# Turning attention probabilities by two row halves of the tensor engine instead of whole blocks

## The chip, the core and the metric

The kernel runs on one of the eight cores of a Trainium2 chip. A core has five engines that run side by side and meet at semaphores: TensorE (PE, with its weight loads listed apart as PEld), VectorE (DVE), ScalarE (ACT), GpSimd (POOL) and SyncE (SP), whose queue issues the DMA transfers here. TensorE multiplies a stationary operand, loaded as weights, with a moving operand and writes into PSUM, which has eight banks of 128 partitions by 512 float32. VectorE and ScalarE read PSUM and write SBUF.

The metric is the device time of one execution in microseconds. Three runs of the kernel before took 1234.39, 1236.35 and 1236.84 us; the median is 1236.35 us.

## What is computed

One layer of a decoder trunk for 1024 tokens of width 1024, batch 1, all in float32: a normalised input goes through one combined projection; a gated delta rule with four heads (mixer A) and a dilated attention with eight heads of 64 (mixer B) run on its columns; both outputs go through one output projection; then a gated MLP with a short convolution and a final norm. The change is in mixer B:

```python
DIL_PATTERNS = ((128, 1), (512, 4), (2048, 16))
for window, dil in DIL_PATTERNS:       # query t sees t, t-d, ..., t-window
    num, den, m = band_attention(stride(qf), stride(kf), stride(vf), window // dil)
# the three branches are merged by their softmax denominators
out = num_tot / den_tot[..., None]
```

So each query sees near keys (its own block of 128 tokens and the block before it), and further keys only where the distance is a multiple of 4 or of 16. The kernel computes the three branches as one softmax with a mask that adds the logarithm of how many branches see a key.

## The kernel before, in words

A small planner (`Weave`) holds the kernel's parts as Python generators with a level each, and a model of when every tile will be ready. `wv.need(...)` tells how long TensorE should do other work before a tile is ready; `wv.run` then always continues the stream of lowest level that is due. The order in which products are recorded is the order in which TensorE executes them (`mm` at L188 and `tp` at L192 stamp it). The planner thereby fills dense projections (`mm3`, three products of 128x512 for each pair of high and low parts of a float32 matrix) between the small pieces of the attention. Each product has a planned duration, an argument of `mm`; a transpose (`tp`) is planned at 0.11 us. Waits that remain on the chip are semaphore waits of the engine in question.

Attention goes over four head pairs (`pi`), two halves of the tokens (`hh`) and, in each, two pairs of query blocks of 128 tokens, so 16 pairs of blocks. In a block, token 4u+c stands at place 32c+u, so a residue class c mod 4 is 32 places in a row. For each pair of blocks `advance` (L1004) runs these steps, the first one for the pair before the current one:

- `turn` (L946): the probabilities `sm` (queries on partitions; the columns are first the far keys, 64 for every two blocks, then 128 or 256 near keys) are transposed, so that keys lie on partitions. Each 128x128 block of `sm` is the stationary operand of one `tp`, and the 128x128 identity the moving one. For each block of the pair and each of two heads there is one PSUM bank, with the near key tiles first and the far key tiles behind. VectorE copies the near part to `pt`; ScalarE copies the far part to `pb`.
- `scores` (L904): products of 64 rows (one head) by queries and near keys, one head in the upper and one in the lower half of the rows, then products with 32 columns for the far keys of each residue class; `softmax` (L929) subtracts the largest, takes exponentials and divides, on VectorE and ScalarE.
- `values` (L966): near probabilities `pt` times the near values `vn`, both heads into the two halves of the bank `po`.
- `merge_classes` (L975), after the second pair: far probabilities `pb`, kept for four blocks, times the far values `vc`, by residue class.

Banks are named by tags with two buffers each: `asc` and `atr` serve scores and transposes, `ch` the outputs `po`, `hf` the dense projections. A new bank of a tag waits for the readers of the bank two turns earlier. Engines take their instructions in order; `uv` and `ua` record VectorE and ScalarE work of the attention at raised priority. While attention runs, TensorE also does the remaining input projections (`dense`, L478: columns `a` and `z`) and the first products of the output projection (`out_proj`, L1069). In the profile, the transposes carry line L193, other products L189, the helper's engine calls L139 and L141.

Of the kernel before, what the change touches and what calls it, by code (L numbers as in the profile page):

```python
# [9 lines left out]
AF = mybir.ActivationFunctionType  # L10
# [5 lines left out]
P = 128  # L16
# [16 lines left out]
TOKEN = "pe"  # L33
# [4 lines left out]
PSLACK = 0.5  # L38
TSLACK = -1.0, -0.6
# [105 lines left out]
def hybrid_layer(tc, I, out):  # L145
    nc = tc.nc
    wv = Weave()
# [3 lines left out]
    uv = Engine(wv, nc.vector, "vector", 0.07, 0.00105, first=tc.high_priority)  # L151
    ua = Engine(wv, nc.scalar, "scalar", 0.12, 0.00085, first=tc.high_priority)
# [10 lines left out]
    def tile_(pool, shape, dt, name, tag, bufs):  # L163
        return wv.slot(pool.tile(list(shape), dt, name=name, tag=tag, bufs=bufs), tag, bufs)
# [12 lines left out]
    def const(name, shape, src=None):  # L177
        t = cp.tile(list(shape), F32, name=name)
        if src is not None:
            sy.dma_start(t, src)  # L180
        return t
# [6 lines left out]
    def mm(dst, lhs, rhs, us, start=True, stop=True, **kw):  # L188
        tc.stamp_issue_order_token(nc.tensor.matmul(dst, lhs, rhs, start=start, stop=stop, **kw).ins, TOKEN)  # L189
        wv.product(us, dst, lhs, rhs)  # L190

    def tp(dst, src):  # L192
        tc.stamp_issue_order_token(nc.tensor.transpose(dst, src, ident).ins, TOKEN)  # L193
        wv.product(0.11, dst, src)

    def mm3(dst, lhs, rhs, first, last, **kw):
        us = 0.2135 * rhs[0].shape[-1] / 512
# [46 lines left out]
    def bank(tag, name="ps"):  # L244
        return tile_(pp_, (P, 512), F32, name, tag, 2)
# [10 lines left out]
    def v8(t):  # L256
        return t.rearrange("p (c t) -> p c t", c=NCH)
# [53 lines left out]
    ident = const("ident", [P, P], I["ident"])  # L311
# [564 lines left out]
    def att_load(pi):  # L876
        qT, kT = [A(nm, "uy") for nm in ("qT", "kT")]
        for i, t in enumerate((qT, kT)):
            sy.dma_start(t, apark[pi, i])
        vn, vc = A("vn", "kt"), A("vc", "kt")  # L880
        cols = slice(pi * P, (pi + 1) * P)
        by_class = vpark.rearrange("(n u c) d -> c u n d", n=NCH, c=4)
        for c in range(4):
            sy.dma_start(v8(vn)[32 * c:32 * c + 32], by_class[c][:, :, cols])
        rows = vpark.rearrange("(b p c) d -> b p c d", b=2, c=4)
        for b in range(2):
            sy.dma_start(vc.rearrange("p (b c d) -> p b c d", b=2, c=4)[:, b], rows[b][:, :, cols])
        return qT, kT, vn, vc

    HALVES = (slice(0, 64), slice(64, 128))  # L890

    def attention():
# [51 lines left out]
                uv.tensor_scalar(sm[:, e, :wd], sm[:, e, :wd], den[:, e:e + 1], None, op0=OP.mult)  # L944

        def turn(pair):  # L946
            pts = A("pt", "dv*", shape=(P, 4, 256))
            for b, (it, tag) in enumerate(zip(pair, ("asc", "atr"))):
                sm, near, far = it["sm"], it["near"], it["far"]
                nf = -(-far // P)  # L950
                it["pt"] = []
                for e in range(2):
                    pt = pts[:, 2 * b + e, :]
                    it["pt"].append(pt)
                    pp = bank(tag)
                    yield wv.need(pp, sm, slack=TSLACK[b])
                    for i in range(near // P):
                        tp(pp[:, i * P:(i + 1) * P], sm[:, e, far + i * P:far + (i + 1) * P])
                    for i in range(nf):
                        tp(pp[:, near + i * P:near + (i + 1) * P], sm[:, e, i * P:(i + 1) * P])  # L960
                    uv.tensor_copy(pt[:, :near], pp[:, :near])
                    if nf:
                        ua.activation(it["pb"][e][:, it["u"], :nf, :].rearrange("p b t -> p (b t)"),
                                      pp[:, near:near + nf * P], AF.Copy)

        def values(pair):  # L966
            yield wv.need(pair[0]["po"], *pair[0]["pt"], slack=-PSLACK)
            for it in pair:
                u = it["u"]
                for i in range(it["near"] // P):  # L970
                    for e, er in enumerate(HALVES):
                        mm(it["po"][er, u * P:(u + 1) * P], v8(it["vn"])[:, it["k0"] // P + i, er],
                           it["pt"][e][:, i * P:(i + 1) * P], 0.11, u == 0 and i == 0, False, skip_group_check=True)

        def merge_classes(g):  # L975
            vcv = g["vc"].rearrange("p (b c d) -> p b c d", b=2, c=4)
            po, hh = g["po"], g["hh"]
            yield wv.need(*g["pb"], slack=-PSLACK)


            parts = (((0, 128, 0), (1, 64, 2)) if hh else ((0, 64, 2),))
            for c in range(4):
                for b, rows, u in parts:
                    for e, er in enumerate(HALVES):
                        mm(po[er].rearrange("p (u t) -> p u t", u=4)[:, u:, 32 * c:32 * c + 32],
                           vcv[:rows, b, c, er], g["pb"][e][:rows, u:, b, 32 * c:32 * c + 32], 0.11 - 0.028 * u,
                           False, c == 3 and b == hh, skip_group_check=True)

        def give(g):
# [14 lines left out]
        def advance(pair):  # L1004
            done = pipe.pop() if pipe else None
            if done is not None:
                yield from turn(done)
            if pair is not None:
                yield from scores(pair)
                pipe.append(pair)  # L1010
            if done is not None:
                yield from values(done)
                if done[1]["u"] == 3:
                    yield from merge_classes(done[0]["g"])
                    give(done[0]["g"])

        for pi in range(4):
            q, k, vn, vc = cur
            for hh in range(2):
                if hh == 1 and pi < 3:  # L1020
                    yield from wv.until(("a", pi + 1, 1))
                    cur = att_load(pi + 1)
                po = bank("ch")
                pb = [A("pb", "qa", shape=(P, 4, 1 + hh, P)) for _ in range(2)]
                if pi == 3 and hh == 1:
                    wv.done.add("last group")
                g = dict(po=po, pb=pb, hh=hh, pi=pi, vc=vc)
                for u in (0, 2):
                    yield from advance([dict(n=4 * hh + i, u=i, q=q, k=k, vn=vn, po=po, pb=pb, g=g)
                                        for i in (u, u + 1)])  # L1030
# [529 lines left out]
```

## Time and profile before

The profiled execution took 1232.33 us; its span from first to last instruction is 1230.2 us.

| | busy us | share of span | instructions |
|---|---|---|---|
| PE (products) | 1206.7 | 98% | 6848 |
| PEld (weight loads) | 992.2 | 81% | 6848 |
| DVE | 948.1 | 77% | 1522 |
| ACT | 570.7 | 46% | 1099 |
| POOL | 47.9 | 4% | 34 |

Busy time counts when at least one instruction of the engine was under way. Products are pipelined and overlap each other: two rows of TensorE may start 0.23 us apart and last 0.39 us each. What a product costs is therefore read from the starts of the products behind it, not from its length. In a row of the timeline the first number is the start in us, the second the length of the group, then engine, line and operation, output <- inputs, the tile of the array in rows*columns (128*128 is the whole array, 64*128 a half of its rows), the moving operand's or result's shape, and the count. A bracket tells how long the engine was idle before and what released it; "issue" means that the profile shows nothing that it waited for. A row of the tile view gives the shortest, middle and longest length in ns, and the first and last start. A row of the waits gives the total in us, the count and the longest.

### The profile page before, as it was taken

To read this page: it belongs to the slowest core of one execution; us is meant where nothing else is said; L and a number is where in the kernel's file an instruction comes from. 1 tells how busy PE (TensorE), PEld (TensorE's weight loads), DVE (VectorE), ACT (ScalarE), POOL (GpSimd) and SP (SyncE) were. 2 spreads that over 40 slices of the span, in tenths; PEclk is the share of its full clock that TensorE was granted. 3 is DMA by queue.
4 is the path that set the end of the run, shared out by engine and by line. 5 is a ranking of instruction groups with operands and counts; after the bars stand their busy time and mean duration, and the time that the engine had idled before them with its cause. 6 is when DMAs were issued, how large, how long until landed. Compare 5 with 4: busy or idle time off the path is not lost.

```text
span 1230.2 us, 17841 instructions
## 1 busy us (share of the span) xinstructions
PE 1206.7 (98%) x6848; PEld 992.2 (81%) x6848; DVE 948.1 (77%) x1522; ACT 570.7 (46%) x1099; POOL 47.9 (4%) x34
## 2 busy tenths in 40 slices
PE   9999999999999998999999999999999999999996
PEld 7878887888877776788888888888888888788886
DVE  7675964566377768577888889889898889899875
ACT  7393344356343345455544445444454553344441
POOL 0211010003100000000000000000000000000000
PEclk9999999999999999999999999999999999999998
DMA  6325251345722403343232231231322397545623
GB/s 231 104 90 154 83 154 71 122 136 167 238 74 95 121 27 111 129 153 117 74 103 88 66 103 61 94 101 53 103 76 79 108 373 254 172 153 183 195 86 137
DMA packets 85798, 155.02 MB, mean 126 GB/s; under 512 B 21168, under 2 KB 36176, under 8 KB 85712
## 3 DMA queue, kind: packets, MB, share of 16 engines
q1 hardware_dynamic: 85712, 153.87, 38.7%
q8 instruction: 54, 0.88, 0.3%
q14 instruction: 32, 0.26, 0.1%
HBM read 117.91 MB, written 35.93 MB: 125 GB/s over the span
## 4 chain that ended last, share of the span: by engine, by line
PE 83%; DVE 9%; DMA 4%; issue 2%; ACT 2%; POOL 0%; SPq 0%; POOLq 0%; DVEq 0%; ACTq 0%
PE ps L189 43%; PE pa L189 18%; PE pc L189 9%; PE dw L189 9%; PE ps L193 3%; DVE pr L139 2%; DMA wd<-in_wd 2%; DMA r<-upark 1%; DVE x1h L139 1%; DVE wd L139 1%; DVE kT L139 1%; DVE sm L141 1%; ACT dec L139 1%; PE warm L189 1%; DVE r L139 0%
## 5 line engine op out<-in xcount | busy, mean ns | idle before, releaser
L189 PE MATMUL dw<-pr 128*128 128x512 f32 (+1 forms) x984 | 213.2, 377 | 2.6 <-DVE x1h L139 1.9
L189 PEld LDWEIGHTS dw<-pr 128*128 128x128 f32 x984 | 176.1, 188 | 38.7 <-DVE x1h L139 3.6
L189 PE MATMUL ps<-xhi,whi 128*128 128x512 f32 x384 | 160.1, 417 | 0.0
L189 PE MATMUL ps<-xhi,wlo 128*128 128x512 f32 x384 | 150.5, 392 | 0.0
L189 PE MATMUL ps<-xlo,whi 128*128 128x512 f32 x384 | 150.1, 391 | 0.0
L189 PE MATMUL pa<-T,pair 128*128 128x512 f32 x528 | 127.0, 389 | 0.0
L189 PEld LDWEIGHTS pa<-T,pair 128*128 128x128 f32 x528 | 99.0, 188 | 20.5
L189 PEld LDWEIGHTS ps<-xhi,wlo 128*128 128x128 f32 x384 | 72.2, 188 | 16.1 <-DVE wlo L139 0.3
L189 PEld LDWEIGHTS ps<-xhi,whi 128*128 128x128 f32 x384 | 72.4, 189 | 14.9 <-issue 2.6
L189 PEld LDWEIGHTS ps<-xlo,whi 128*128 128x128 f32 x384 | 72.6, 189 | 11.2
L139 ACT ACTIVATE u<-pa 128x512 f32<-128x512 f32 x44 | 26.3, 598 | 110.7 <-PE pa L189 110.7
L139 DVE SCALAR_TENSOR_TENSOR y<-xu,fcw,y 128x1023 f32<-128x1023 f32 (+1 forms) x44 | 56.4, 1281 | 25.7 <-ACT y L139 25.6
L139 ACT ACTIVATE whi<-wst 128x1024 fp32r<-128x1024 f32 (+2 forms) x42 | 42.9, 1022 | 69.7 <-PE ps L189 64.1
L141 ACT ACTIVATE sm<-sm,mx 128x320 f32<-128x320 f32 (+4 forms) x64 | 36.1, 565 | 63.1 <-DVE mx L141 63.1
L189 PE MATMUL pc<-B,pair 128*128 128x512 f32 x264 | 63.4, 389 | 0.0
L189 PE MATMUL pa<-B,A 128*128 128x512 f32 x264 | 63.4, 389 | 0.0
L189 PE MATMUL pc<-T,S 128*128 128x512 f32 x264 | 63.4, 389 | 0.0
L189 PE MATMUL pa<-T,S 128*128 128x512 f32 x264 | 63.4, 389 | 0.0
L139 DVE TENSOR_TENSOR wst<-wst 128x512 f32<-128x512 f32 x88 | 60.4, 687 | 0.7
L189 PE MATMUL ps<-B,pair 128*128 128x512 f32 x252 | 60.5, 389 | 0.0
L139 DVE TENSOR_TENSOR wlo<-wst,whi 128x1024 fp32r<-128x1024 f32 (+2 forms) x42 | 49.4, 1175 | 12.1 <-ACT whi L139 12.0
L189 PEld LDWEIGHTS pa<-B,A 128*128 128x128 f32 x264 | 49.6, 188 | 10.3
(237 smaller groups left out, 2347.9 us busy)
## 6 DMA issues: line engine op xcount, KB each, us to landing
wst<-in_wu SPq DMA_DIRECT2D x44, 512.0 KB, 3.8
wd<-in_wd SPq DMA_DIRECT2D x44, 512.0 KB, 3.9
upark<-y SPq DMA_DIRECT2D x22, 512.0 KB, 3.8
wst<-in_wi SPq DMA_DIRECT2D x21, 512.0 KB, 3.7
r<-upark SPq DMA_DIRECT2D x11, 512.0 KB, 8.0
r<-upark SPq DMA_DIRECT2D x22, 256.0 KB, 7.0
wa<-in_wd SPq DMA_DIRECT2D x22, 256.0 KB, 2.8
wst<-in_wv SPq DMA_DIRECT2D x8, 512.0 KB, 3.6
```

The lines of the kernel that those rows point to most:

```text
L139: return getattr(eng, op)(*a, **kw)
L141: return getattr(eng, op)(*a, **kw)
L189: tc.stamp_issue_order_token(nc.tensor.matmul(dst, lhs, rhs, start=start, stop=stop, **kw).ins, TOKEN)
L193: tc.stamp_issue_order_token(nc.tensor.transpose(dst, src, ident).ins, TOKEN)
```

## The change

In `turn`, each transpose of a 128x128 block becomes two transposes with 64 rows: the upper and the lower 64 queries of the block, each with the matching 64x64 part of the identity, one after the other. The two halves write two banks, one per query half; a bank now holds both heads, with the key tiles of each. So two banks are taken at once and filled together, where each bank was filled for one head and copied before. A half is planned at 0.055 us. VectorE copies from each bank the near tiles of both heads for 64 queries. ScalarE copies each far tile of a bank by itself, both heads together. `pb` becomes one tile for each far key tile with both heads in it, where it was one tile for each head with both key tiles; `merge_classes` indexes it accordingly. `tp` takes the identity part and the planned time as arguments.

```diff
-    def tp(dst, src):
-        tc.stamp_issue_order_token(nc.tensor.transpose(dst, src, ident).ins, TOKEN)
-        wv.product(0.11, dst, src)
+    def tp(dst, src, idt=None, us=0.11):
+        tc.stamp_issue_order_token(nc.tensor.transpose(dst, src, ident if idt is None else idt).ins, TOKEN)
+        wv.product(us, dst, src)
...
         def turn(pair):
-            pts = A("pt", "dv*", shape=(P, 4, 256))
+            pts = A("pt", "dv*", shape=(P, 2, 2, 256))
             for b, (it, tag) in enumerate(zip(pair, ("asc", "atr"))):
-                sm, near, far = it["sm"], it["near"], it["far"]
-                nf = -(-far // P)
-                it["pt"] = []
+                sm, near, far, u = it["sm"], it["near"], it["far"], it["u"]
+                nn, nf = near // P, -(-far // P)
+                pt = it["pt"] = pts[:, b]
+                pps = [bank(tag) for _ in range(2)]
+                yield wv.need(*pps, sm, slack=TSLACK[b])
+                pvs = [pp.rearrange("p (e i t) -> p e i t", e=2, t=64) for pp in pps]
                 for e in range(2):
-                    pt = pts[:, 2 * b + e, :]
-                    it["pt"].append(pt)
-                    pp = bank(tag)
-                    yield wv.need(pp, sm, slack=TSLACK[b])
-                    for i in range(near // P):
-                        tp(pp[:, i * P:(i + 1) * P], sm[:, e, far + i * P:far + (i + 1) * P])
+                    for i in range(nn + nf):
+                        o = far + i * P if i < nn else (i - nn) * P
+                        for pv, rr in zip(pvs, HALVES):
+                            tp(pv[:, e, i, :], sm[rr, e, o:o + P], ident[rr, rr], 0.055)
+                for pv, rr in zip(pvs, HALVES):
+                    uv.tensor_copy(pt.rearrange("p e (i t) -> p e i t", t=P)[:, :, :nn, rr], pv[:, :, :nn, :])
                     for i in range(nf):
-                        tp(pp[:, near + i * P:near + (i + 1) * P], sm[:, e, i * P:(i + 1) * P])
-                    uv.tensor_copy(pt[:, :near], pp[:, :near])
-                    if nf:
-                        ua.activation(it["pb"][e][:, it["u"], :nf, :].rearrange("p b t -> p (b t)"),
-                                      pp[:, near:near + nf * P], AF.Copy)
+                        rows = P
+                        ua.activation(it["pb"][i][:rows, :, u, rr], pv[:rows, :, nn + i, :], AF.Copy)
...
-                           vcv[:rows, b, c, er], g["pb"][e][:rows, u:, b, 32 * c:32 * c + 32], 0.11 - 0.028 * u,
+                           vcv[:rows, b, c, er], g["pb"][b][:rows, e, u:, 32 * c:32 * c + 32], 0.11 - 0.028 * u,
...
-                pb = [A("pb", "qa", shape=(P, 4, 1 + hh, P)) for _ in range(2)]
+                pb = [A("pb", "qa", shape=(P, 2, 4, P)) for _ in range(1 + hh)]
```

More of the change, by code (lines that the diff above doesn't have):

```diff
@@ L946, in turn @@
         def turn(pair):
-            pts = A("pt", "dv*", shape=(P, 4, 256))
+            pts = A("pt", "dv*", shape=(P, 2, 2, 256))
             for b, (it, tag) in enumerate(zip(pair, ("asc", "atr"))):
-                sm, near, far = it["sm"], it["near"], it["far"]
-                nf = -(-far // P)
-                it["pt"] = []
-                for e in range(2):
-                    pt = pts[:, 2 * b + e, :]
-                    it["pt"].append(pt)
-                    pp = bank(tag)
-                    yield wv.need(pp, sm, slack=TSLACK[b])
-                    for i in range(near // P):
-                        tp(pp[:, i * P:(i + 1) * P], sm[:, e, far + i * P:far + (i + 1) * P])
-                    for i in range(nf):
-                        tp(pp[:, near + i * P:near + (i + 1) * P], sm[:, e, i * P:(i + 1) * P])
-                    uv.tensor_copy(pt[:, :near], pp[:, :near])
-                    if nf:
-                        ua.activation(it["pb"][e][:, it["u"], :nf, :].rearrange("p b t -> p (b t)"),
-                                      pp[:, near:near + nf * P], AF.Copy)
+                sm, near, far, u = it["sm"], it["near"], it["far"], it["u"]
[4 more added lines that the diff above has]
+                pvs = [pp.rearrange("p (e i t) -> p e i t", e=2, t=64) for pp in pps]
+                for e in range(2):
+                    for i in range(nn + nf):
[4 more added lines that the diff above has]
+                    uv.tensor_copy(pt.rearrange("p e (i t) -> p e i t", t=P)[:, :, :nn, rr], pv[:, :, :nn, :])
+                    for i in range(nf):
+                        rows = P
+                        ua.activation(it["pb"][i][:rows, :, u, rr], pv[:rows, :, nn + i, :], AF.Copy)
         def values(pair):
-            yield wv.need(pair[0]["po"], *pair[0]["pt"], slack=-PSLACK)
+            yield wv.need(pair[0]["po"], pair[0]["pt"], slack=-PSLACK)
             for it in pair:
@@ L972, in values @@
                         mm(it["po"][er, u * P:(u + 1) * P], v8(it["vn"])[:, it["k0"] // P + i, er],
-                           it["pt"][e][:, i * P:(i + 1) * P], 0.11, u == 0 and i == 0, False, skip_group_check=True)
+                           it["pt"][:, e, i * P:(i + 1) * P], 0.11, u == 0 and i == 0, False, skip_group_check=True)
         def merge_classes(g):
```

## The prediction, made before the changed kernel ran

> **What bounds the kernel now.** I read the page first: the span, the busy shares and the chain that ended last.
>
> ```profile
> span 1230.2 us, 17841 instructions
> PE 1206.7 (98%) x6848; PEld 992.2 (81%) x6848; DVE 948.1 (77%) x1522; ACT 570.7 (46%) x1099; POOL 47.9 (4%) x34
> PE 83%; DVE 9%; DMA 4%; issue 2%; ACT 2%; POOL 0%; SPq 0%; POOLq 0%; DVEq 0%; ACTq 0%
> ```
>
> TensorE is busy for 98% and carries 83% of the chain. Next the sums by stretch, over the attention stage (the softmax tiles `sm` live from 329 to 485 us) and over three parts of it.
>
> ```profile
> 325.00:495.00 170.00, 164.58 (x1507) 126.22 (x1506) 122.28 (x336) 70.45 (x196) 0.00 (x0) 0.99 0.30 95
> 345.00:365.00 20.00, 20.00 (x203) 15.65 (x204) 14.83 (x40) 8.77 (x25) 0.00 (x0) 1.00 0.19 66
> 445.00:465.00 20.00, 20.00 (x177) 15.28 (x176) 13.89 (x42) 7.12 (x22) 0.00 (x0) 1.00 0.12 34
> 465.00:485.00 20.00, 18.24 (x190) 13.15 (x188) 16.89 (x43) 11.92 (x29) 0.00 (x0) 1.00 0.23 78
> ```
>
> The columns are length, busy PE, PEld, DVE, ACT, POOL, granted clock, DMA share. In the stretches 345 to 365 and 445 to 465 us, as in all between, PE has no free time at full clock, because dense projections fill between the attention pieces; DVE has 5 to 6 of 20 us free. What PE gains or loses there moves the end one for one. Only the stage's start and its last 20 us hold real waits. Now the instructions the change touches, by tile:
>
> ```profile
> L193 PEld LDWEIGHTS ps<-ident,sm x184: 138/140/231, 332.2 to 484.7; 128*128 128x128 f32 x184
> L193 PE MATMUL ps<-ident,sm x184: 270/272/446, 332.4 to 484.8; 128*128 128x128 f32 x184
> L141 DVE COPY pt<-ps x64: 267/417/429, 334.2 to 487.0; 128x256 f32<-128x256 f32 x56, 128x128 f32<-128x128 f32 x8
> L141 ACT ACTIVATE pb<-ps x48: 259/278/387, 341.3 to 487.5; 128x128 f32<-128x128 f32 x32, 128x256 f32<-128x256 f32 x16
> L189 PE MATMUL ps<-pb,vc x192: 218/267/324, 347.5 to 490.3; 64*64 64x64 f32 x128, 128*64 128x128 f32 x64
> ```
>
> **The change part by part. Turning, inside a batch.** 184 transposes of 128 rows become 368 of 64 rows, in pairs of an upper and a lower half. A batch of eight before, from the timeline, with the dense products (xhi, xlo by whi, wlo) round it:
>
> ```profile
> 440.58 0.40 PE L189 MATMUL ps<-xhi,wlo 128*128 128x512 f32 x1
> 440.58 1.03 PEld L193 LDWEIGHTS ps<-ident,sm 128*128 128x128 f32 x8
> 440.81 1.04 PE L193 MATMUL ps<-ident,sm 128*128 128x128 f32 x8
> 441.58 0.19 PEld L189 LDWEIGHTS ps<-xhi,whi 128*128 128x128 f32 x1
> 441.60 0.47 PE L189 MATMUL ps<-xhi,whi 128*128 128x512 f32 x1
> 441.92 0.39 PE L189 MATMUL ps<-xlo,whi 128*128 128x512 f32 x1
> 442.14 0.40 PE L189 MATMUL ps<-xhi,wlo 128*128 128x512 f32 x1
> ```
>
> Dense products start 0.23 us apart (441.92 to 442.14). The batch begins 0.23 after the dense product ahead, its first load already running at 440.58, so going in is free. The dense product behind starts at 441.60 but lasts 0.47 instead of 0.39, so it really begins at 441.68: eight transposes hold PE for 0.87, 0.109 each, 20.1 us for all 184. Going out is free too.
>
> What sets 0.109: a load of 128 columns, or the 128 moving columns? And do two row halves run together? Two more places:
>
> ```profile
> 38.21 0.51 PE L189 MATMUL ps<-sel,barow 128*128 128x8 f32 x4
> 38.22 0.41 PEld L189 LDWEIGHTS ps<-sel,barow 128*128 128x128 f32 x3
> ...
> 344.52 0.40 PE L189 MATMUL ps<-xhi,wlo 128*128 128x512 f32 x1
> 344.85 0.30 PEld L189 LDWEIGHTS ps<-kT,qT 64*128 64x128 f32 x4 [0.37 <-issue]
> 344.96 0.41 PEld L189 LDWEIGHTS ps<-kT,qT 64*128 64x128 f32 x4
> ...
> 446.44 0.39 PE L189 MATMUL ps<-xhi,wlo 128*128 128x512 f32 x1
> 446.76 0.52 PEld L189 LDWEIGHTS ps<-kT,qT 64*128 64x128 f32 x8 [0.35 <-issue]
> 446.76 0.93 PE L189 MATMUL ps<-kT,qT 64*128 64x128 f32 x8
> ```
>
> The gate products move 8 columns only, yet their loads of 128 columns stand (0.41 − 0.19) / 2 = 0.11 apart: the load alone costs 0.11. The scores' near products (`kT,qT 64*128`) have the very shape of the new transposes' loads, two row halves into two banks. Four of their loads start within 0.30 − 0.19 = 0.11, so they go in pairs, and the pairs follow 0.11 apart; eight loads take 0.52, four pairs at 0.11 and the last one's length. So a pair of half-height transposes costs 0.109, bound by its load, although it moves 64 columns where one moved 128. Inside a batch nothing is gained: 0.0 us. The bounds are 0.058 a pair (next fence), a gain of 184 × 0.051 = 9.4 us, and 0.218 where the halves took turns, a loss of 20.1 us. I take 0.109, the only row with this load.
>
> [...]
>
> **Entering and leaving half-height work.** Before, batches cost nothing at their edges. Half-height ones will. In: after the dense product at 446.44 the next would start at 446.67; the half-height load starts at 446.76, with its product, which must then wait 0.11 for the load: 0.09 + 0.11 = 0.20 us (344.52 to 344.85 gives 0.21). Out:
>
> ```profile
> 347.54 0.54 PEld L189 LDWEIGHTS ps<-pb,vc 64*64 64x64 f32 x16 [0.17 <-issue]
> 347.54 0.68 PE L189 MATMUL ps<-pb,vc 64*64 64x64 f32 x16
> 348.15 0.50 PE L189 MATMUL ps<-xhi,whi 128*128 128x512 f32 x1
> ```
>
> Sixteen class products of 64x64 end at 348.22; one lasts 0.218 (the row above), so the last starts at 348.00. (The loads end at 348.08; eight pairs of them are 0.058 apart.) The dense product starts at 348.15 and lasts 0.50, 0.11 over its usual 0.39: really 348.26. That is 0.26 from the last short product to dense work, where a full-height transpose needed 0.109: 0.15 more. A batch between dense products thus loses 0.20 + 0.15 = 0.35 us.
>
> The planned order of the changed kernel has 31 batches: two for each of 16 turns, the last two in one. 28 stand between dense products on both sides: 28 × 0.35 = 9.8 us. Three have other small-tile work on one side, where a switch existed already, and pay about one edge: 3 × 0.15 = 0.5 us. The bounds for an edge are nothing (the full-height rows) and 0.21. That PE really loses these switches is seen in the waits of the stage:
>
> ```profile
> PEld ps L189 <- issue: 17.5, 67, 0.4
> PE ps L193 <- DVE sm L141: 2.8, 3, 1.8
> PEld ps L189 <- ACT pb L141: 2.1, 3, 1.2
> PEld ps L189 <- DVE pt L141: 1.8, 1, 1.8
> ```
>
> 67 times the loader stood idle with nothing to wait for: that fits 16 turns with about four changes of tile shape each. The change adds some 60.
>
> **Copies and the values.** VectorE still makes 64 `pt` copies of the same sizes: 0. ScalarE has 64 copies of 128 columns for 48: 64 × 0.278 − (32 × 0.278 + 16 × 0.387) = +2.7 us, on an engine busy 70 of 170 us; what hides it is PE's dense work, and it shows only where scores wait for a bank that a `pb` copy frees (2.1 us above). Both banks of a batch are now filled together, so the first copy starts about half a batch, 0.3 to 0.4 us, later, and the values that much later. The cover: the planned order puts nine dense products instead of six (0.7 us more) between a pair's second batch and the next scores. At the end of the stage that cover is missing and I count +0.5 us. Class products keep number and size and read the rows of one key tile unbroken: 0. `pb` takes three ring buffers a head pair instead of four; no DMA is added on SP's queue and nothing on POOL's.
>
> **The end of the stage.** Order there changes as well:
>
> ```profile
> 483.97 1.06 PE L193 MATMUL ps<-ident,sm 128*128 128x128 f32 x8 [0.65 <-DVE sm L141]
> 485.56 1.22 DVE L139 SCALAR_TENSOR_TENSOR zz<-zz,xr 128x1024 f32<-128x1024 f32 x1
> 486.70 0.75 DVE L141 COPY pt<-ps 128x256 f32<-128x256 f32 x2
> 487.17 0.87 PE L189 MATMUL ps<-pt,vn 128*64 128x128 f32 x7 [1.55 <-DVE pt L141]
> ```
>
> Before, the last copies sit behind a gate product of 1.22 us on VectorE and PE idles 1.55. In the changed order the last four copies follow each other, and twelve dense products instead of six stand before the last batch. But ScalarE's splits of the mixer outputs now stand among the last exponentials, and several of them wait for a DMA, with the exponentials queued behind. I take −1.5 us of the roughly 4 us of waits, between −4 and +3.
>
> **Sum:** 0.0 + 9.8 + 0.5 + 0.5 − 1.5 = +9.3 us. The profiled execution took 1232.33 us (span 1230.2), 4.0 under the median of 1236.35, and would become 1241.6; against the median I predict 1245.6 us.
>
> **The rivals.**
> 1. The halves are truly independent (ends faster). A half's load runs ahead beside the other half's product, across a batch's edge too: pairs at 0.058, no edges, −9.4 us, 1227.0 us. For it: loads of the pair do run together, and 64x64 products reach 0.058. Against: 0.058 belongs to loads of 64 columns, and no half-height load in the rows starts before the dense product ahead is out. With pairs at 0.058 it beats the old kernel by 0.2% once an edge pair costs under (9.4 − 2.5) / 31 = 0.22 us; the rows say 0.35.
> 2. Pairs at 0.058, but the edges paid: 10.3 − 9.4 = +0.9 us, 1237.3 us, no change that can be told. For and against it stand the rows of rival 1, without the edges. [...]
> 3. The halves take turns (both read the same identity tile): +20.1 + 10.3 − 1.5 + 0.5 = +29.4, 1265.8 us. Against it: the pairs at 344.85.
>
> **How the numbers follow.** Forecast 0.78, rival 1 0.09, rival 2 0.09, rival 3 0.04. 0.2% (2.5 us) is about what a measurement of this kernel can tell from no change; so faster 0.09, same 0.09, slower 0.82. The forecast's own range is 1240 to 1250: the end of the stage from −4 to +3 moves it to 1243 to 1250, edges a quarter cheaper take another 2.6 off. The range for 8 in 10 reaches down over rival 2, to 1234.5, and up to 1251; rivals 1 and 3 (0.13) stay outside.
>
> **What would show it.** In the changed profile: 368 `ident,sm` records of 64 rows in pairs 0.109 apart; the first dense product behind each batch 0.50 long; no load of a batch before the dense product ahead of it is through; the stage longer by some 9 us, everything after it of equal length; idle "issue" of the loader up by some 60 times. The forecast is wrong if pairs stand 0.06 or 0.22 apart, if dense follows a batch at once, or if the last 20 us of the stage gain or lose more than 4 us.

## The result and the profile after

The changed kernel took 1242.37 us (median of 16 runs, 1238.01 to 1247.19) against 1234.49 for the kernel before in the same session (16 runs, 1232.64 to 1237.27). The ratio is 1.0061, 95% interval 1.0050 to 1.0072: about 7.5 us slower. The forecast was +9.3 us and 1245.6 us. Sign, size and range held, but, as will be seen, one term of the sum was 8.6 us too high and another about 7 us too low.

The page of the changed kernel, with its span, its engines and the chain that ended last:

```profile
span 1242.6 us, 18211 instructions
PE 1212.2 (98%) x7032; PEld 987.4 (79%) x7032; DVE 949.3 (76%) x1522; ACT 570.4 (46%) x1115; POOL 47.4 (4%) x34
PE 80%; DVE 8%; DMA 7%; ACT 3%; issue 2%; SPq 0%; POOL 0%; POOLq 0%; DVEq 0%; ACTq 0%
```

The profiled execution took 1244.76 us, 2.4 above the median. A second one of the same kernel (below) took 1239.17.

The tile view of the changed kernel, for the rows that answer those shown of before:

```profile
L193 PEld LDWEIGHTS ps<-ident,sm x368: 134/139/226, 333.4 to 498.4; 64*128 64x128 f32 x184
L193 PE MATMUL ps<-ident,sm x368: 221/223/366, 333.4 to 498.5; 64*128 64x64 f32 x184
L141 DVE COPY pt<-ps x64: 277/417/428, 335.1 to 499.1; 128x256 f32<-128x256 f32 x56, 128x128 f32<-128x128 f32 x8
L141 ACT ACTIVATE pb<-ps x64: 259/278/302, 343.7 to 499.7; 128x128 f32<-128x128 f32 x64
```

368 half-height transposes stand where 184 were, the copies cost what they did (417 ns for 417, 278 for 278), and the last transpose starts at 498.5 us instead of 484.8. One batch of six pairs from the timeline of the changed kernel:

```profile
438.20 0.39 PE L189 MATMUL ps<-xhi,wlo 128*128 128x512 f32 x1
438.52 0.45 PEld L193 LDWEIGHTS ps<-ident,sm 64*128 64x128 f32 x12 [0.35 <-issue]
438.52 0.59 PE L193 MATMUL ps<-ident,sm 64*128 64x64 f32 x12
439.04 0.50 PE L189 MATMUL ps<-xhi,whi 128*128 128x512 f32 x1
439.37 0.40 PE L189 MATMUL ps<-xlo,whi 128*128 128x512 f32 x1
```

Six pairs of loads take 0.45, the last load 0.139: pairs stand (0.45 − 0.139) / 5 = 0.062 apart, not 0.109. The edges are as foreseen: the first load starts 0.32 behind the dense product ahead (438.52 for 438.20), later than another dense product would have started (0.23 behind, 438.43), and the dense product behind lasts 0.50, so it really begins at 439.15. From 438.43 to 439.15 the batch holds TensorE for 0.72 us: 6 × 0.062 + 0.35. Six whole transposes would have held it for 6 × 0.109 = 0.65. TensorE's own bill for all of it is 184 × 0.062 + 31 × 0.34 = 21.9 us for the 20.1 before: **+1.9 us**, far less than the 7.5 measured. So something else costs more than the changed instructions. The stretches of the changed kernel (columns as in the prediction, with GB/s last) show where:

```profile
445.00:465.00 20.00, 20.00 (x200) 14.33 (x199) 14.09 (x41) 8.15 (x26) 0.00 (x0) 1.00 0.12 41
465.00:485.00 20.00, 15.51 (x189) 11.01 (x188) 17.81 (x41) 12.96 (x29) 0.00 (x0) 0.97 0.46 141
485.00:500.00 15.00, 13.17 (x140) 9.07 (x140) 11.68 (x31) 7.54 (x25) 0.00 (x0) 0.93 0.19 60
```

In the middle PE is full, as before. Between 465 and 485 us it works 15.5 us instead of 18.2, and after that the granted clock is below 1. In the timeline of the changed kernel that is one wait, what VectorE and ScalarE do meanwhile, and what follows it:

```profile
479.19 0.68 PE L189 MATMUL ps<-pb,vc 64*64 64x64 f32 x16
479.86 1.22 DVE L139 TENSOR_TENSOR og<-og,zz 128x1024 f32<-128x1024 f32 x1
481.12 1.06 ACT L139 ACTIVATE ohi<-og 128x1024 fp32r<-128x1024 f32 x1 [0.25 <-DVE og L139]
483.45 0.82 PE L193 MATMUL ps<-ident,sm 64*128 64x64 f32 x12 [3.59 <-DVE sm L141]
484.21 0.79 PE L189 MATMUL ps<-ohi,whi 128*128 128x512 f32 x1
484.80 0.63 PE L189 MATMUL ps<-olo,whi 128*128 128x512 f32 x1
485.23 0.63 PE L189 MATMUL ps<-ohi,wlo 128*128 128x512 f32 x1
```

Class products are followed directly by a batch of transposes that waits 3.6 us for `sm`: no dense product stands between them. Among the steps of that softmax stand work on a mixer output (`og`, 1.22 us) and its split (`ohi`, 1.06). Behind it dense products start 0.43 apart instead of 0.23 and last 0.63 instead of 0.39. The waits view of the changed kernel from 325 to 510 us, total, count, longest:

```profile
PEld ps L189 <- issue: 16.6, 64, 0.4
PEld ps L193 <- issue: 15.9, 27, 3.7
PE ps L193 <- DVE sm L141: 6.8, 4, 3.6
ACT ohi L139 <- DMA ot<-mixer: 4.6, 3, 2.8
```

Transposes wait 6.8 us for `sm`, where they waited 2.8. The loader's 27 idle times at L193, where the kernel before has one (2.1 us), are mostly the batches' leading edges, 0.35 us each, with a few waits such as the long one among them.

By landmarks, from the first scores to the last output-projection product before the MLP the kernel before takes 249.8 us (328.7 to 578.5), the changed one 256.1 (329.6 to 585.7), in its second profile 254.6. From the first down-projection product to the last it is 216.9 before, 220.1 in the first profile after and 217.1 in the second: so most of that 3 us was that execution's.

### The profile page after: what moved, and what is told of

The parts are those of the page before. It is cut to its first block, busy times and chain, and to the rows that moved or that the text cites. A ratio compares the mean times of both kernels' runs of the same rounds, so it can differ in the third digit from the quotient of the medians.

```text
span 1242.6 us, 18211 instructions
## 1 busy us (share of the span) xinstructions
PE 1212.2 (98%) x7032; PEld 987.4 (79%) x7032; DVE 949.3 (76%) x1522; ACT 570.4 (46%) x1115; POOL 47.4 (4%) x34
## 4 chain that ended last, share of the span: by engine, by line
PE 80%; DVE 8%; DMA 7%; ACT 3%; issue 2%; SPq 0%; POOL 0%; POOLq 0%; DVEq 0%; ACTq 0%
PE ps L189 42%; PE pa L189 19%; PE pc L189 9%; PE dw L189 6%; DMA wd<-in_wd 3%; DMA r<-upark 3%; PE ps L193 2%; DVE pr L139 2%; DVE x1h L139 1%; DVE kT L139 1%; DVE wd L139 1%; DVE olo L139 1%; ACT dec L139 1%; PE warm L189 1%; DVE sm L141 1%
## 5 line engine op out<-in xcount | busy, mean ns | idle before, releaser
L139 ACT ACTIVATE pr<-wd 128x1024 fp32r<-128x1024 f32 x33 | 35.0, 1060 | 56.5 <-DVE wd L139 37.1
```

What stands on the lines that cost most here:

```text
L139: return getattr(eng, op)(*a, **kw)
```

## The experiments

The theories at the start. **M**: a transpose's pitch comes from its moving columns, so a pair costs 0.06 and the edges 0.35, and the rest of the loss is in waits. **S**: those waits come from the planner's new order, because a batch that fills both banks at once is planned to end later, so that nine dense products stand where six did and the dense products have run out when the stage ends. **E**: the half-height batches cost more than the rows show, whatever the order. Times are medians, ratios against the kernel before in the same session with their 95% interval.

**1. The pitch by itself.** Behind the last instruction of the kernel before stand, twice, short rows of TensorE work on one tile, with six dense products (`mfill`) between them: eight whole transposes, eight pairs of halves, eight upper halves followed by eight lower, and the same loads as ordinary float32 products.

```diff
+        for i in range(8):
+            for t, rr in ((a, UP), (b, LO)):
+                tr(t[:, (i % 8) * 64:(i % 8 + 1) * 64], rstdB[rr, i * P:(i + 1) * P], ident[rr, rr])
+        fill(6)
...
+            mm(a[:, (i % 8) * 64:(i % 8 + 1) * 64], rstdB[:, i * P:(i + 1) * P], ident[:, :64], 0.2)
...
+                mm(t[:, (i % 8) * 64:(i % 8 + 1) * 64], rstdB[rr, i * P:(i + 1) * P], ident[rr, rr], 0.2)
```

> The kernel before, with rows of small TensorE work added behind its last instruction, each row between dense fill products, twice: eight full-height transposes (full128), eight pairs of half-height transposes taken in turn (halfpair), the same with eight uppers and then eight lowers (halfrow), eight full-height float32 products with 128 weight columns and 64 moving ones (prod64), and such products as half-height pairs (halfprod). The added work is not part of the layer and lengthens the execution by some 40 us. Theory M (a transpose is paced by its moving columns, its load is quicker than an ordinary float32 load): full128 0.109 us each, halfpair 0.06 a pair, halfrow 0.06 each, so 0.12 for an upper and its lower; prod64 0.11 a pass and halfprod 0.11 a pair of passes, held by the ordinary load. Theory L (the prediction's: the load of 128 columns paces every one): halfrow 0.11 each, prod64 and halfprod 0.11. Theory R (only the pairing of row halves makes them quick): halfpair 0.06, halfrow 0.11 each.

The timeline of this kernel (start, length, shape, count):

```profile
1235.08 1.03 PEld L1511 LDWEIGHTS full<-ident,rstdB 128*128 128x128 f32 x8
1236.11 1.62 PE L189 MATMUL mfill<-md 128*128 128x512 f32 x6
1237.66 0.57 PEld L1511 LDWEIGHTS halfpair<-ident,rstdB 64*128 64x128 f32 x16 [0.35 <-issue]
1238.30 1.66 PE L189 MATMUL mfill<-md 128*128 128x512 f32 x6
1239.89 0.88 PEld L1511 LDWEIGHTS halfrow<-ident,rstdB 64*128 64x128 f32 x16 [0.37 <-issue]
1242.34 1.89 PE L189 MATMUL prod<-ident,rstdB 128*128 128x64 f32 x16
1245.60 2.00 PE L189 MATMUL halfprod<-ident,rstdB 64*128 64x64 f32 x32
```

Whole transposes stand 0.11 apart (the eight products take 1.04 us, the last 0.27 of it: 0.77 / 7), pairs (0.57 − 0.14) / 7 = 0.06. An ordinary float32 product is recorded as two passes, each with its load (16 records for eight products); with the same 64 moving columns the passes stand (1.89 − 0.27) / 15 = 0.11 apart, and pairs of half-height ones (2.00 − 0.27) / 15 = 0.115. The gate products in the prediction, with 8 moving columns, stand 0.11 apart too. So the load of 128 columns does set 0.11 for a pass of an ordinary product, whether 64 or 128 rows high, but not for a half-height transpose, whose load has the same shape. M is right on the pitch of a pair; that whole transposes are held at 0.11 by their 128 moving columns fits, but no run moves fewer columns at full height. Eight pairs hold TensorE for 0.84 from the place of the next dense product, eight whole transposes for 0.89. A pair saves 0.05 and a batch's edges cost 0.34 to 0.36, so halves break even at seven pairs; 16 of the 31 batches here have six, six have eight, one sixteen and eight fewer. Two rows of halves (`halfrow`) take 0.88 where pairs take 0.57: (0.88 − 0.14) / 15 = 0.05 for each half. A half-height transpose is thus quick by itself, which neither theory L (the prediction's) nor R allows, with 0.11 each, and taking an upper and a lower half in turn brings the two from 0.10 to 0.06.

**2. Everything but the halves.** The new layout, both banks taken at once, 64 copies on ScalarE, but whole transposes:

```diff
-                        for pv, rr in zip(pvs, HALVES):
-                            tp(pv[:, e, i, :], sm[rr, e, o:o + P], ident[rr, rr], 0.055)
+                        tp(pps[e][:, i * P:(i + 1) * P], sm[:, e, o:o + P])
```

> The changed kernel with full-height transposes again: two banks still taken together, all transposes of a block before the first copy, pt and pb in the new layout with 64 copies on ScalarE; only the row halves are undone, and the banks hold one head each. If the layout and ScalarE's 16 more copies are free, it is the kernel before: 1234.5 us, within 0.2%. If the copies cost, up to 2.7 us more: 1237. If the banks taken together make the loss, it stays at 1242.

1233.08 us, 1.0001 (0.9990 to 1.0011). The order of TensorE comes out as before. The layout and ScalarE's sixteen more copies cost nothing, as predicted.

**3 and 4. The order alone.** The changed kernel with six dense products before the scores again (experiment 3), and the kernel before with nine to twelve (experiment 4), each by one argument of the planner:

```diff
-            yield wv.need(*pair[0]["ps"], *pair[1]["ps"], pair[0]["q"], pair[0]["k"])
+            yield wv.need(*pair[0]["ps"], *pair[1]["ps"], pair[0]["q"], pair[0]["k"], slack=-0.7)
...
-            yield wv.need(*pair[0]["ps"], *pair[1]["ps"], pair[0]["q"], pair[0]["k"])
+            yield wv.need(*pair[0]["ps"], *pair[1]["ps"], pair[0]["q"], pair[0]["k"], slack=0.7)
```

> The changed kernel, with the scores asked for 0.7 us earlier by the planner, so that six dense products and not nine stand between a pair's second batch of transposes and the next scores, as in the kernel before; all instructions are the same. Theory S (dense work runs out before the stage ends, because 0.7 us more of it is spent on each pair): the wait of 3.6 us and the slow clock behind it go, and what is left is edges (+10.3) less quicker pairs (-8.3): 1236.5 us, to 1238 if the scores then wait for copies. Theory E (the edges make the loss, order does not matter): 1242.

> The kernel before, with the scores asked for 0.7 us later, so that nine to twelve dense products stand where six stood; no instruction is changed. Theory S: dense work runs out early here too, PE waits near the stage's end, 3 to 6 us slower: 1238 to 1240. Theory E: no change, 1234.5.

Experiment 3: 1237.69 us, 1.0039 (1.0027 to 1.0051). The 3.6 us wait is gone and the time is what S expects, but waits of 1 to 2 us remain, and behind the last of them 26 class products take 3.19 us in its profile, where 31 take 2.64 in that of experiment 2. Experiment 4: 1241.95 us, 1.0070 (1.0054 to 1.0085), slower by 8.6 us with not one instruction changed, more than the 3 to 6 expected. Its timeline at the stage's end:

```profile
474.64 2.17 PE L193 MATMUL ps<-ident,sm 128*128 128x128 f32 x12 [4.43 <-DVE sm L141]
476.46 0.78 PE L189 MATMUL ps<-ohi,whi 128*128 128x512 f32 x1
477.04 0.63 PE L189 MATMUL ps<-olo,whi 128*128 128x512 f32 x1
...
496.74 1.94 PE L193 MATMUL ps<-ident,sm 128*128 128x128 f32 x8 [4.26 <-DVE sm L141]
498.34 0.78 PE L189 MATMUL ps<-ohi,whi 128*128 128x512 f32 x1
```

The same picture as in the changed kernel, with whole transposes: dense products spent early are missing at the end, and each long wait is followed by slow products. So order alone can cost all of the loss; whether it did here, the last experiments tell.

**5. A better order for the whole transposes.** Experiment 2 with `slack=-0.3` in `scores`.

> The partner of the six-product kernel with the row halves undone: full-height transposes, banks taken together, the new layout, and an order of dense products that is nearly that of e3_six (scores asked for 0.3 us earlier; twelve dense products before the last batch instead of nine). By the pitches measured in e1 (a batch of n pairs costs 0.34 + 0.062 n in halves and 0.111 n whole), the 31 batches with 184 transposes cost 1.5 to 1.9 us more in halves: this kernel should take 1.5 to 2 us less than e3_six, less again by e3_six's wait of 1.8 us in the middle of the stage: 1233.5, the kernel before. If halves cost nothing once the order is right, it equals e3_six: 1237.7.

1230.17 us, 0.9967 (0.9955 to 0.9979), 4 us faster than the kernel before, the fastest of this study, and 3 us below what was expected. In its profile the transposes wait 2.4 us for `sm` and the values 0.8 for `pt` (2.8 and 1.6 before).

**6, 7 and 8. Fewer edges.** Both blocks of a pair in one batch, so 16 batches instead of 31; with halves (6), with halves and more dense products ahead of the scores (7), and as 6 with whole transposes (8). By the pitch, 6 should beat 8 by 184 × 0.0485 − 16 × 0.34 = 3.5 us.

```diff
-            for b, (it, tag) in enumerate(zip(pair, ("asc", "atr"))):
+            banks = [[bank(tag) for _ in range(2)] for tag in ("asc", "atr")]
+            yield wv.need(*banks[0], *banks[1], pair[0]["sm"], pair[1]["sm"], slack=-1.4)
+            for b, (it, pps) in enumerate(zip(pair, banks)):
...
-                pps = [bank(tag) for _ in range(2)]
-                yield wv.need(*pps, sm, slack=TSLACK[b])
```

> The changed kernel with both blocks of a pair turned in one batch: 16 batches instead of 31, each up to 32 half-height transposes, all four banks asked for together (1.4 us ahead of the second block's softmax), the scores asked for 1.0 us earlier. By e1's pitches 16 x 0.34 + 184 x 0.062 = 16.9 us against 20.4 whole: if edges are what the halves cost, this is 3.5 us less than its partner e8_joined_whole, and some 3 us under the kernel before, 1230, where it finds no new wait: three dense products (0.7 us) between a joined batch and the next scores are few, four copies of 0.42 us follow the batch. If these waits are paid by PE, up to 1 us a pair: 1240.

> As e6_joined, but the scores asked for 0.7 us earlier only, so that six dense products stand between a joined batch and the scores; dense work ends earlier (12 products fewer are left behind the stage). If waits for the copies weigh more than dense work running out: faster than e6_joined by 1 to 3 us. If the end of the stage weighs more: slower by 1 to 3.

> The partner of e6_joined: both blocks in one batch of full-height transposes, same asking times, an order of dense products that differs at a few places only. Theory M and the edges: 3.5 us slower than e6_joined. If half-height pairs were no quicker in the kernel than whole ones: 5.5 us faster than e6_joined (16 edges of 0.34 saved).

Measured: 1237.96 us, 1.0036 (1.0023 to 1.0049); 1239.15 us, 1.0038 (1.0023 to 1.0053); 1237.41 us, 1.0023 (1.0010 to 1.0036). A miss: halves do not win by 3.5, they are level or a little slower. (The orders of dense products in 6 and 8 are not quite the same; 7 is as slow as 6, so its dense products moved ahead of the scores bring nothing.) The timelines of 6 and then of 8 at the same place:

```profile
484.78 1.12 PE L193 MATMUL ps<-ident,sm 64*128 64x64 f32 x16 [4.70 <-DVE sm L141]
486.17 1.12 PE L193 MATMUL ps<-ident,sm 64*128 64x64 f32 x16 [0.27 <-DVE sm L141]
487.21 0.79 PE L189 MATMUL ps<-ohi,whi 128*128 128x512 f32 x1
487.81 0.63 PE L189 MATMUL ps<-olo,whi 128*128 128x512 f32 x1
```

```profile
485.82 3.31 PE L193 MATMUL ps<-ident,sm 128*128 128x128 f32 x16 [4.70 <-DVE sm L141]
488.88 0.48 PE L189 MATMUL ps<-ohi,whi 128*128 128x512 f32 x1
489.20 0.40 PE L189 MATMUL ps<-olo,whi 128*128 128x512 f32 x1
```

The same wait, and then the same slowness (granted clock 0.51 from 484.7 to 490.0 us in 6, 0.66 from 485.7 to 490.0 in 8): 16 whole transposes take 3.3 us there instead of 1.9. But with halves the slowness goes on over six dense products.

**9, 10 and 11. Halves and order crossed.** Halves in the exact order of before, by planning each pair as one whole transpose (9, partner 2); halves in the order of experiment 5 (10, partner 5: as 9, with `slack=-0.3`); whole transposes in the exact order of the changed kernel (11, partner: the changed kernel).

```diff
-                            tp(pv[:, e, i, :], sm[rr, e, o:o + P], ident[rr, rr], 0.055)
+                            tc.stamp_issue_order_token(
+                                nc.tensor.transpose(pv[:, e, i, :], sm[rr, e, o:o + P], ident[rr, rr]).ins, TOKEN)
+                        wv.product(0.11, pps[e], sm)
...
+                        tc.stamp_issue_order_token(
+                            nc.tensor.transpose(pps[e][:, i * P:(i + 1) * P], sm[:, e, o:o + P], ident).ins, TOKEN)
+                        for pp in pps:
+                            wv.product(0.055, pp, sm)
```

> The changed kernel's instructions, half-height pairs and all, but planned as if the transposes were whole, so that TensorE's order is that of the kernel before, item for item (partner: e2_whole, 1.0001 of the kernel before). Theory M + edges: TensorE itself pays 31 x 0.34 - 184 x 0.0485 = 1.6 to 1.9 us more; the first copies come 0.3 to 0.4 us later with six dense products for cover: 1.9 us over the kernel before, 1236, up to 1239 if scores or values wait for the copies. Rival (halves as such make the whole loss): 1241 to 1242.

> The same in e5_sixfull's order, item for item (partner: e5_sixfull, 0.9967 of the kernel before). Theory M + edges: 1.6 to 1.9 us over e5_sixfull: 0.998 of the kernel before, up to 1.000 with waits for copies. Rival: 7 to 8 us over it, 1.003.

> Full-height transposes in the changed kernel's order, item for item (partner: the changed kernel, 1.0061 of the kernel before). If the order makes the larger part of the loss: 1.6 to 1.9 us under the changed kernel, so 1.0045 of the kernel before, 1239. If the halves make it: 1.000.

Ratios to the kernel before:

| order | whole | halves | halves cost |
|---|---|---|---|
| of before | 1.0001 (exp. 2) | 1.0055, 1.0035 to 1.0074 (exp. 9) | 0.54% |
| of exp. 5 | 0.9967 (exp. 5) | 1.0004, 0.9992 to 1.0016 (exp. 10) | 0.37% |
| of the changed kernel | 1.0021, 1.0010 to 1.0031 (exp. 11) | 1.0061 (the change) | 0.40% |

Two misses for S: 9 was expected at 1236 to 1239 us and took 1240.28; 11 should have kept most of the loss and kept a third. Experiment 10 took a little more than expected too (1.0004 for 0.998 to 1.000). The order costs 0.20%, 2.5 us, and the halves 0.37 to 0.54%, 4.6 to 6.7 us, in every order. That is more than their bill of 1.9 us, as E said. But E's mechanism, dearer batches, is not in the rows. Where two kernels have the same order, the start of the same product can be compared. First experiment 2, then 9, before the first batch and before the waits at the end of the stage:

```profile
331.87 0.39 PE L189 MATMUL ps<-xhi,wlo 128*128 128x512 f32 x1
478.65 1.09 PE L189 MATMUL ps<-pt,vn 128*64 128x128 f32 x16
```

```profile
332.20 0.39 PE L189 MATMUL ps<-xhi,wlo 128*128 128x512 f32 x1
480.73 1.09 PE L189 MATMUL ps<-pt,vn 128*64 128x128 f32 x16
```

All batches but the last ones lie between, and the halves fall behind by 2.08 − 0.33 = 1.8 us. In the same way experiment 10 falls behind 5 by 1.9 us, and the changed kernel (its second profile) behind 11 by 1.8. So the bill of 1.9 us holds in all three orders, and E is wrong on the batches; what halves cost beyond it comes later than 475 to 481 us.

**What the missing 3 to 5 us are.** One part is longer waits for copies at the end of the stage: the values there wait 1.55 us for `pt` in experiment 2 and 2.21 in 9, 0.76 in 5 and 0.47 + 1.14 in 10. Another part is the clock. The windows of experiment 9 behind its waits show the granted clock (third number from the end):

```profile
484.00:487.30 3.30, 1.61 (x33) 1.19 (x30) 3.30 (x8) 2.56 (x7) 0.00 (x0) 1.00 0.00 0
487.30:490.70 3.40, 1.90 (x18) 1.45 (x18) 2.58 (x4) 1.57 (x5) 0.00 (x0) 0.50 0.73 211
490.70:494.10 3.40, 3.40 (x27) 2.06 (x26) 2.55 (x3) 2.13 (x4) 0.00 (x0) 0.50 0.73 257
494.10:497.50 3.40, 3.40 (x9) 2.63 (x9) 2.50 (x4) 1.50 (x4) 0.00 (x0) 0.50 0.62 189
```

The clock is halved for three periods of 3.4 us, where its partner's profile (2) has none at that place (1.00 from 475 to 510 us). Each run records its mean granted clock; span × (1 − clock) is taken as the time lost to it, an estimate, 3.5 to 5 us of it at the end of the profiles, where TensorE has next to nothing left to do (busy for 0.63 of the last 7.6 us in the changed kernel's). Means over all runs, against the kernel before in the same session (5.6 to 5.7 us lost):

| kernel | runs | time | of it clock | rest |
|---|---|---|---|---|
| 2 whole, old order | 12 | +0.2 | +0.4 | −0.2 |
| 9 halves, old order | 6 | +6.9 | +5.6 | +1.3 |
| 5 whole, order of 5 | 8 | −4.1 | +0.4 | −4.5 |
| 10 halves, order of 5 | 11 | +0.7 | +2.1 | −1.4 |
| 11 whole, new order | 11 | +2.5 | +2.1 | +0.4 |
| the change | 16 | +7.2 | +3.4 | +3.7 |
| 3 the change, six | 12 | +4.7 | +2.3 | +2.4 |
| 4 before, nine to twelve | 6 | +8.5 | +4.5 | +4.0 |
| 6 joined halves | 8 | +4.1 | +4.6 | −0.5 |
| 7 as 6, more dense products | 6 | +4.7 | +4.7 | 0.0 |
| 8 joined whole | 12 | +3.1 | +2.5 | +0.6 |

(The clock's share has a standard error of 0.5 to 0.9 us, the rest of 0.3 to 0.6. For the change the clock of the runs beside it is not recorded; the 5.65 of the other sessions, 67 runs, is taken. Between runs of one kernel the time moves 0.92 us for 0.001 of clock, where 1.24 would be a full effect, so the clock's column is an upper figure by up to a quarter.)

With the clock taken out, halves cost 1.5 us in the old order, 3.0 in that of experiment 5, 3.4 in the new one, and gain 1.0 when joined, where the bill says +1.9, +1.9, +1.9 and −3.5. The first agrees with the bill; 1.1, 1.5 and 2.5 us in the others lie beyond it, with standard errors of 0.7 to 0.8. The clock takes 1.3 to 5.2 us more from each kernel with halves than from its partner.

The profiles show where the rest can lie. From the first scores to the last output-projection product halves cost 5.5 us in the old order (248.7 to 254.2), 1.9 in that of experiment 5 (246.5 to 248.4) and 2.2 and 3.7 in the new one (252.4 to 254.6 and 256.1). In experiment 10 that is no more than the bill; but its down projection, which the change does not touch, is 2.7 us longer (215.6 to 218.3). That projection takes 215.3 to 218.3 us in seven profiles with whole transposes and 216.4 to 220.1 in seven with halves, so whether halves lengthen it is not shown.

**12. The changed kernel once more**, for a second profile.

> The changed kernel once more, for a second profile. Its first profile was 2.4 us above its median, and 3.1 us of its loss stood in the last projection (from the first to the last dw product 220.1 us, before 216.9), which the change does not touch. If that is the run's own: 216 to 218 us here and the same stage of attention and output projection, 256.1 us from the first scores to the last product (before 249.8). If the change causes it: 219 to 221 again.

1239.17 us, beside 1232.47 for the kernel before. The stage's wait of 3.6 us and the slow products behind it are there again; the 3 us in the down projection and the slow stretch near 600 us are not.

## Why the prediction came out as it did

- **Inside a batch, 0.0 us: wrong.** The first failed step is "the load alone costs 0.11 … so a pair of half-height transposes costs 0.109, bound by its load". The row was that of ordinary float32 products, and for these experiment 1 confirms it (0.11). Half-height transposes' loads go in pairs 0.06 apart; what held whole ones at 0.109 were then most likely their 128 moving columns, which no run tests by itself. The term was −184 × 0.047 = −8.6 us, near its lower bound of −9.4.
- **Edges, +10.3 us: right.** 0.34 to 0.36 a batch against 0.35 predicted, in the changed kernel and in experiment 1, with the signs named: the first dense product 0.50 long, no load ahead of time.
- So far that is rival 2: +1.9 us by the rows, for its +0.9, and the same-order pairs confirm it. It had a chance of 0.09, and alone it would have made 1236 to 1238 us.
- **Copies, 0: right** (experiment 2).
- **Later copies +0.5, order −1.5, together −1.0: wrong in sign and size.** 7.5 − 1.9 = +5.6 us came on top of the bill. Experiment 11 gives 2.5 of them to the order alone; the other 3.1 come with the halves beyond their bill, as 4.8 and 2.7 do in experiments 9 and 10. The second failed step is "the planned order puts nine dense products instead of six" taken as a cover. These products are not free: they are drawn from the dense work that fills the end of the stage. With the cover already spent, the class products at 479 us are followed by transposes that wait 3.6 us. The prediction named the splits of the mixer outputs among the exponentials, which do stand there, but set more against them; the waits for a DMA that it also named are no longer than before (4.6 us for 4.5). The wait it wanted removed, 1.55 us for `pt`, did go. The later copies themselves cost 0.7 to 0.9 us at the end of the stage in experiments 9 and 10.
- **What the sum had no term for:** the clock after a wait. At most 3.4 of the 5.6 us are lost there, up to 2.1 of these with the order alone (experiment 11). The other 2.2 or more are waits and what stays unexplained.
- **"Issue" idle times up by some 60: wrong**, up by 23, from 68 to 91. Only the leading edge of a batch shows as idle time of the loader (0.35 us); the trailing one shows as a longer product (0.50 for 0.39).
- **Everything after the stage of equal length: only within the scatter.** The MLP's up phase took 424.7 and 423.3 us in two profiles, 422.3 before, with one period of half clock in the first; the down projection is treated above.
- **The prediction's own signs.** One of the three that it named against itself came, pairs 0.06 apart, and another nearly: the stage became 6.3 and 4.8 us longer in the two profiles, for some 9 foreseen, and less the bill of 1.9 its end lost 4.4 and 2.9, where more than 4 was the sign.

So the forecast was right by luck: an error of −8.6 us and one of +6.6 cancelled. Of the 3.2 us between 1245.6 and the median of 1242.37, 1.9 are not the sum's at all: the forecast stood on a median of 1236.35 from three runs, where 16 runs gave 1234.49. The reasoning that would have given the right sum had rival 2's pitch and a price for the end of the stage. The bounds of the pitch were in the text and the value taken was at the wrong one; for copies and order, +5.6 lay outside the stated +3.5 (+0.5 and +3).

## What to carry to other kernels

Take the pitch of an instruction from a row of the same operation, a transpose's from transposes: two loads of the same shape cost 0.115 us in a pair of product passes and 0.06 in a pair of transposes. Running two row halves side by side saves TensorE time here only in batches of more than seven pairs, because going in and out of half-height work costs 0.35 us a batch and a pair saves 0.05; even joined batches of up to sixteen did not make the kernel faster (1.0036 for 1.0023). And where a planner fills gaps from a fixed supply of dense work, a cover used early is a wait later: one argument moved the time by −4 (experiment 5 against 2) to +8.6 us (experiment 4) without changing an instruction.

## What the runs showed of the hardware

In the trace of the changed kernel the granted clock changes on a fixed grid. It goes to one half at four places; the windows of 1 us in which it changes:

```profile
343.00:344.00 1.00, 1.00 (x13) 0.64 (x13) 1.00 (x5) 0.27 (x1) 0.00 (x0) 0.88 0.00 0
483.00:484.00 1.00, 0.55 (x12) 0.58 (x12) 1.00 (x4) 1.00 (x4) 0.00 (x0) 0.85 0.76 213
599.00:600.00 1.00, 0.60 (x2) 0.56 (x3) 1.00 (x3) 0.64 (x2) 0.00 (x0) 0.88 0.00 0
1234.00:1235.00 1.00, 0.06 (x1) 0.06 (x2) 0.11 (x1) 0.00 (x0) 0.70 (x1) 0.82 0.00 0
```

A mean of 0.85 with a clock of 1 and then 0.5 puts the change at 483.70, and the others at 343.76, 599.76 and 1234.64. The first halved period ends at 347.17 (0.64 granted from 347.10 to 347.20), so it lasts 3.41 us. The distances between the four changes are 139.94, 116.06 and 634.88 us: 41, 34 and 186 times 3.413. The stretches around one of them:

```profile
480.30:483.70 3.40, 0.24 (x8) 0.28 (x8) 3.40 (x10) 3.15 (x8) 0.00 (x0) 1.00 0.85 270
483.70:487.10 3.40, 3.40 (x17) 2.21 (x13) 3.40 (x8) 2.31 (x6) 0.00 (x0) 0.50 0.42 151
487.10:490.50 3.40, 3.10 (x25) 2.10 (x25) 2.54 (x6) 1.03 (x4) 0.00 (x0) 1.00 0.65 202
```

A cell of 3.4 us in which TensorE had little to do (0.24 busy) is followed here by one at half clock, which costs up to 1.7 us, half of its length, even though TensorE is busy in it (3.40 of 3.40). Half clock need not follow a wait: in experiment 9 the period behind 490.7 us was full of half-width class products (PE busy 3.40 of 3.40), and the next one was still at half clock. Nor need the period ahead be empty: before the changes at 343.76 and 599.76 us TensorE was busy for 1.68 and 2.64 of 3.40 us, and in experiment 9 half clock first follows a window with 1.61 us busy of 3.30, while its partner, with 1.75 busy in the same window, kept the full clock. For a sum this means, as an estimate from these cells, that a wait of a few us may cost 1.7 us or more on top of its own length, depending on where the grid lies in that execution. In the second profile of the changed kernel it lies elsewhere: the half clock at the stage's wait begins at 481.1 us there (0.68 granted from 479.90 to 483.30), 2.6 us earlier, which is not a whole number of periods of 3.41. That would also let executions of one kernel differ by a few us.

What stays open: why kernels with half-height transposes lose more clock than their partners even in the same order, and the 1 to 2.5 us beyond bill and clock. That longer waits at the end of the stage leave emptier cells would fit experiment 9, but no run here separates it from where the grid happens to lie.
